# Rotary embedding from cached tables on one core: one of three table copies goes from GpSimd to ScalarE

## The chip, the cores and the metric

One core of a Trainium2 chip. The metric is the device time of one execution in microseconds; the median of several runs is quoted. In the profile, PE is TensorE (PEld its weight loads), DVE is VectorE, ACT is ScalarE, POOL is GpSimd and SP is SyncE. A line number such as L109 is a line of that kernel's source. The change adds one line, so L161 of the kernel before is L162 after it, while L106 to L159 are the same in both.

## The reference

```python
# x: (8, 8, 1024, 64) float32; cos, sin: (1024, 32) float32
half = x.shape[-1] // 2
x_first, x_second = x[..., :half], x[..., half:]
out_first  = x_first * cos - x_second * sin
out_second = x_first * sin + x_second * cos
return concatenate([out_first, out_second], axis=-1)
```

About 17 MB come in and 17 MB go out, with four products and two sums for each pair of elements.

## The kernel before

The input is cut into eight units of 128 partitions x 64 rows x 64 elements (2 MB each). For most units ScalarE stages a piece of x into PSUM, VectorE multiplies it with both tables at once, and GpSimd or TensorE forms the sums; SyncE issues the stores.

The part that matters here is the start. The tables are 1024 rows long. A partition needs 64 of them, an even and an odd block of 32 rows, and the pattern repeats every 16 partitions. In the tile `tb` the odd blocks (rows `H:`) are made for the first 32 partitions by a shuffle, and the same 32 x 2048 numbers are then copied to the other three groups of 32 partitions (the quadrants). The even blocks are spread by TensorE into PSUM (`en` for sin, `ec` for cos), and unit 0's first half is computed straight from there.

```python
for part, r in ((en[:, :BK], rs[:, :BK]), (en[:, BK:], rs[:, BK:]),
                (ec[0], rc[:, :BK]), (ec[1], rc[:, BK:])):
    nc.tensor.matmul(part, sel, r, start=True, stop=True)
odd = [2 * (i % (Q // 2)) + 1 for i in range(Q)]
for t, r in ((sn, rs), (cs, rc)):
    nc.vector.stream_shuffle(t[0:Q, H:], flat(r), odd)
for k in range(1, P // Q):                                   # L160: three copies on GpSimd
    nc.gpsimd.tensor_copy(out=tb4[k * Q:(k + 1) * Q, H:], in_=tb4[0:Q, H:])   # L161
mul(nc.vector, rows(sv[0], 0, H), rows(xt[0], 0, H), tab(flat(en), 0, H))     # x * sin
for i in range(2):                                                            # x * cos
    mul(nc.vector, rows(sv[7], i * G, (i + 1) * G), rows(xt[0], i * G, (i + 1) * G),
        tab(flat(ec[i]), 0, G))
pool_sums(0, 0, H, sv[7])        # GpSimd: reads the sin and the cos products (L109, L110)
stage(pre, 0, H, R)              # ScalarE: second half of unit 0 into PSUM (L113)
nc.scalar.copy(out=sn[:, :H], in_=flat(en))
# ... cos likewise ...
products(pre, 0, H, R)           # VectorE: reads the odd blocks (L106)
pool_sums(0, H, R)               # GpSimd: reads that product
# ... units 1 to 7; in the traces POOL's instructions start in this order ...
```

## Time and profile before

| | before |
|---|---|
| median, lowest to highest of 3 runs | 85.48 us, 85.44 to 85.49 |
| span of the profiled run | 83.3 us |
| busy: DVE, POOL, ACT | 68.5, 69.0, 38.8 us |
| three copies on POOL (L161) | 5.7 us, 1888 ns each |
| POOL's last sum ends | 75.4 us |
| last store lands (issued at 75.88, 6.4 us to landing) | about 82.3 us |

Read it in this order. The busy shares and the 40 slices say which engines are full and when. The chain that ended last says what the profile takes for the path. The order of instructions in a short stretch then shows what really follows on what: the time at which an instruction starts, set against the ends of everything that it reads. The lines themselves are in the prediction below.

### The profile page before, as it was taken

The page shows a single profiled execution, that of the slowest core. Times are in us where ns is not written, and L with a number is a line of the kernel's source. Part 1 is how long each engine was busy: PE and PEld are TensorE (multiplying, and loading weights), DVE is VectorE, ACT ScalarE, POOL GpSimd, SP SyncE. Part 2 cuts the span into 40 slices and gives each one's busy share as a digit, 9 for nine tenths or more (in the row PEclk, how much of TensorE's full clock was granted, in tenths as well). Part 3 has the DMA queues.
Part 4 walks back from the last instruction along what each step waited for, and adds up shares of the span by engine and source line. Part 5 has one row for each costly group of instructions (what it writes and reads, how often), then busy time and mean ns, then how long its engine had stood idle before and what let it go on. Part 6 is the DMA issues. An engine that isn't in the chain of part 4 may idle for free.

```text
span 83.3 us, 386 instructions
## 1 busy us (share of the span) xinstructions
PE 44.0 (53%) x80; PEld 16.9 (20%) x80; DVE 68.5 (82%) x30; ACT 38.8 (47%) x35; POOL 69.0 (83%) x37
## 2 busy tenths in 40 slices
PE   0199930003992694949869494970994970000000
PEld 0143300002440332404233240410430510000000
DVE  0193999999999999999999999999999998950000
ACT  4400795364068548196176856665356627000000
POOL 3009989999999999999999999999999999992000
PEclk9999999999999999999999999999579999755555
DMA  2999999899998999989999999999999999998991
GB/s 35 291 421 456 433 401 480 378 480 401 401 480 378 496 385 409 472 378 496 370 409 472 393 472 409 433 433 401 480 393 464 417 417 448 401 472 373 425 414 71
DMA packets 2832, 33.82 MB, mean 406 GB/s; under 512 B 336, under 2 KB 336, under 8 KB 784
## 3 DMA queue, kind: packets, MB, share of 16 engines
q1 hardware_dynamic: 2784, 33.69, 96.1%
q10 hardware_dynamic: 48, 0.13, 0.4%
HBM read 17.04 MB, written 16.78 MB: 406 GB/s over the span
## 4 chain that ended last, share of the span: by engine, by line
POOL 66%; issue 11%; PE 5%; DMA 4%; DVE 3%; POOLq 2%
POOL w L110 26%; POOL w L109 24%; POOL w L106 14%; PE en L156 5%; DMA w<-in_sin_cached_dram 4%; DVE w L106 3%; POOL tb L161 2%; POOLq L257 2%; POOLq L109 0%; POOLq L106 0%
## 5 line engine op out<-in xcount | busy, mean ns | idle before, releaser
L106 DVE TENSOR_TENSOR w<-st,tb 128x3072 f32<-128x3072 f32 (+2 forms) x19 | 54.7, 2956 | 0.3 <-ACT st L113 0.3
L113 ACT COPY st<-w 128x1536 f32<-128x1536 f32 (+1 forms) x19 | 24.9, 1310 | 15.7 <-DVE w L106 14.8
L183 PE MATMUL acc<-w,plus 128*128 128x512 f32 x36 | 21.3, 677 | 20.4 <-ACT w L189 11.5
L109 POOL TENSOR_TENSOR w<-w 128x1024 f32<-128x1024 f32 (+3 forms) x11 | 23.8, 2165 | 0.2
L110 POOL TENSOR_TENSOR w<-w 128x1024 f32<-128x1024 f32 (+3 forms) x11 | 23.8, 2163 | 0.0
L183 PEld LDWEIGHTS acc<-w,plus 128*128 128x128 f32 x36 | 7.0, 215 | 33.8 <-ACT w L189 18.1
L189 ACT COPY w<-acc 128x1024 f32<-128x1024 f32 x9 | 9.1, 1010 | 8.4 <-PE acc L184 8.4
L106 POOL TENSOR_TENSOR w<-w,tb 128x1280 f32<-128x1280 f32 x4 | 11.6, 2902 | 0.2
L184 PE MATMUL acc<-w,minus 128*128 128x512 f32 x18 | 10.8, 686 | 0.0
L161 POOL COPY tb<-tb 32x2048 f32<-32x2048 f32 x3 | 5.7, 1888 | 5.2 <-DVE tb L159 5.1
L184 PE MATMUL acc<-w,plus 128*128 128x512 f32 x18 | 9.2, 592 | 0.0
L156 PE MATMUL en<-w,sel 32*128 32x512 f32 x4 | 3.7, 1089 | 3.9 <-DMA w<-in_sin_cached_dram 3.9
L184 PEld LDWEIGHTS acc<-w,minus 128*128 128x128 f32 x18 | 4.0, 223 | 5.4 <-issue 5.4
L113 ACT COPY pre<-w 128x2048 f32<-128x2048 f32 x1 | 1.9, 1870 | 5.9 <-DMA w<-in_x_dram 5.9
L106 DVE TENSOR_TENSOR w<-pre,tb 128x4096 f32<-128x4096 f32 x1 | 4.4, 4418 | 0.0
L184 PEld LDWEIGHTS acc<-w,plus 128*128 128x128 f32 x18 | 3.4, 190 | 4.3 <-issue 4.3
L156 PE MATMUL ec<-w,sel 32*128 32x512 f32 x4 | 3.6, 1056 | 0.0
L106 DVE TENSOR_TENSOR w<-w,en 128x2048 f32<-128x2048 f32 x1 | 2.3, 2289 | 1.4 <-PE en L156 1.4
L159 DVE LOAD_MASK_SELECT tb<-w x2 | 0.0, 8 | 3.8 <-DMA w<-in_sin_cached_dram 3.8
L109 POOL TENSOR_TENSOR w<-w,w 128x1024 f32<-128x1024 f32 x1 | 2.3, 2340 | 0.3 <-POOL tb L161 0.3
L159 DVE STREAM_SHUFFLE tb<-w 32x1024 f32<-32x1024 f32 x2 | 2.5, 1278 | 0.0
L106 DVE TENSOR_TENSOR w<-w,ec 128x1024 f32<-128x1024 f32 x2 | 2.4, 1218 | 0.0
(17 smaller groups left out, 12.4 us busy)
## 6 DMA issues: line engine op xcount, KB each, us to landing
w<-in_x_dram SPq DMA_DIRECT2D x7, 2048.0 KB, 24.8
out_dram<-w SPq DMA_DIRECT2D x7, 2048.0 KB, 10.3
w<-in_x_dram SPq DMA_DIRECT2D x2, 1024.0 KB, 6.2
out_dram<-w SPq DMA_DIRECT2D x2, 768.0 KB, 6.4
out_dram<-w SPq DMA_DIRECT2D x1, 512.0 KB, 6.4
w<-in_cos_cached_dram ACTq DMA_DIRECT2D x1, 128.0 KB, 3.4
w<-in_sin_cached_dram SPq DMA_DIRECT2D x1, 128.0 KB, 3.0
```

Source lines behind the costliest of these rows:

```text
L106: eng.tensor_tensor(out=o, in0=a, in1=t, op=TT.mult)
L109: eng.tensor_tensor(out=o[:, :, 0], in0=c[:, :, 0], in1=s[:, :, 1], op=TT.subtract)
L110: eng.tensor_tensor(out=o[:, :, 1], in0=c[:, :, 1], in1=s[:, :, 0], op=TT.add)
L113: nc.scalar.copy(out=pt[:, :(n1 - n0) * hd], in_=xt[u][:, n0 * hd:n1 * hd])
L156: nc.tensor.matmul(part, sel, r, start=True, stop=True)
L159: nc.vector.stream_shuffle(t[0:Q, H:], flat(r), odd)
L161: nc.gpsimd.tensor_copy(out=tb4[k * Q:(k + 1) * Q, H:], in_=tb4[0:Q, H:])
L183: nc.tensor.matmul(a[:, k], plus, xr[:, :, k], start=True, stop=False)
L184: nc.tensor.matmul(a[:, k], plus if k else minus, sr[:, :, 1 - k], start=False, stop=True)
L189: nc.scalar.copy(out=rows(xt[u], n0, n0 + G), in_=a)
L257: with _tile.TileContext(nc) as tc:
```

## The change

Its intent is to take 1.9 us from GpSimd, which is as full as any engine, and give it to ScalarE, which is idle half of the time.

```diff
         for t, r in ((sn, rs), (cs, rc)):
             nc.vector.stream_shuffle(t[0:Q, H:], flat(r), odd)
-        for k in range(1, P // Q):
+        nc.scalar.copy(out=tb4[Q:2 * Q, H:], in_=tb4[0:Q, H:])
+        for k in range(2, P // Q):
             nc.gpsimd.tensor_copy(out=tb4[k * Q:(k + 1) * Q, H:], in_=tb4[0:Q, H:])
```

## The prediction

> **What bounds the kernel now.** I read the page first (engine shares, the 40 slices, the chain), then the busy time by stretch, then the order of the instructions between 3 and 17 us, where the change lies. The page's engine and slice lines:
>
> ```profile
> PE 44.0 (53%) x80; PEld 16.9 (20%) x80; DVE 68.5 (82%) x30; ACT 38.8 (47%) x35; POOL 69.0 (83%) x37
> DVE  0193999999999999999999999999999998950000
> POOL 3009989999999999999999999999999999992000
> DMA  2999999899998999989999999999999999998991
> ```
>
> DVE and POOL are both full from about 8 us to about 75 us, and DMA is full from 2 us to 81 us. Three resources are tied, so 83% on POOL alone doesn't make POOL the bound. The chain that ended last does name POOL (66% of the span), and it holds one piece of the line that changes:
>
> ```profile
> 7.68 2.54 DVE w L106 x2
> 10.23 0.04 issue
> 10.27 1.90 POOL tb L161
> 12.17 0.29 issue
> 12.46 0.03 POOL w L109
> ```
>
> This reads as if the third POOL copy (L161) were on the path. The trap is the 0.29 us of "issue" behind it: the copy has ended at 12.17, and POOL still starts its next work only at 12.46. So something else lets it go. The view of that line (L109) between 5 and 14 us has it:
>
> ```profile
> L109 POOLq EVENT_SEMAPHORE  x2: 17/2940/5863, 6.5 to 12.5; - x2
> its engine sat idle before it (us, times) until:
>   POOL tb L161: 0.3, 1
> ```
>
> POOL's sequencer sits in one semaphore wait for 5.863 us from 6.5 us, that is until about 12.37, and a second one of 17 ns follows. If the copies' end (12.17) were the last thing awaited, the long wait would be over by about 12.2. What does end just before 12.37 is on DVE:
>
> ```profile
> 7.68 2.29 DVE L106 TENSOR_TENSOR w<-w,en 128x2048 f32<-128x2048 f32 x1 [1.42 <-PE en L156]
> 9.88 2.43 DVE L106 TENSOR_TENSOR w<-w,ec 128x1024 f32<-128x1024 f32 x2
> 12.23 4.42 DVE L106 TENSOR_TENSOR w<-pre,tb 128x4096 f32<-128x4096 f32 x1
> ```
>
> 9.88 + 2.43 = 12.31 us is the end of the two products by cos, and L109 is the sum that reads exactly these (the compiled order shows L109 waiting on a DVE semaphore as well as on POOL's own). 12.31 plus about 0.06 is 12.37. The view's "POOL tb L161" is an inferred releaser; the times speak for DVE.
>
> The end of the run has a second lock. Busy POOL time, DMA share and rate by stretch, from 44 us on:
>
> ```profile
> 44.00:48.00 4.00, 4.00 (x4) 1.00 0.96 410
> 52.00:56.00 4.00, 4.00 (x3) 1.00 1.01 430
> 64.00:68.00 4.00, 4.00 (x2) 1.00 0.97 414
> 72.00:75.40 3.40, 3.40 (x2) 0.50 0.97 414
> 75.40:81.40 6.00, 0.03 (x1) 0.50 0.99 413
> ```
>
> Columns: the stretch, its length, POOL's busy time, the granted clock, DMA share, GB/s. DMA never falls below 0.96 although stores come only as the sums finish. After POOL has ended (75.4), DMA works 6 us more at its full rate. It moves 413 GB/s x 6.0 us = 2.48 MB there (and about 0.08 MB in the tail), while the two stores not yet issued at 75.4 are 768 KB and 512 KB, 1.31 MB. So some 1.25 MB, about 3 us, of older stores are still queued when POOL delivers its last sum.
>
> **What the Trainium skill says.** "ScalarE: Activation LUTs", section "What ACT_TABLE_LOAD costs": an instruction with immediate scale and bias takes 186 ns + 0.833 ns per element of the row, 1892 ns at 2048. The trace agrees: ACT's 128x2048 copy takes 1870 ns. "GPSIMD Engine Reference", section "Engine selection": one-input work on POOL is roughly line-rate, so ACT should not be a faster copier. It agrees: L161 takes 1888 ns for 32x2048. "SBUF — State Buffer", section "SBUF: two separate sides": DVE and GpSimd share one port pair, ACT has its own; a DVE operation with two SBUF inputs can be blocked by POOL. No such block shows here: DVE's products have one input in PSUM, and the 1024-wide product takes 1218 ns beside POOL's copy and 1222 to 1224 ns beside POOL's sums. "DMA: Bandwidth & Descriptors", section "Where 436 GB/s comes from": a ceiling of 435 GB/s for the 16 engines. The trace holds 410 to 446 GB/s in every stretch that I read between 6.4 and 75 us, at about that ceiling; the page's lower HBM limit, about 358, doesn't show.
>
> **The change part by part.** Removed from POOL: one of three copies of 32x2048, 1.89 us. The order stays otherwise the same: on POOL two copies and then the same 28 sums and products. POOL's copies would run from 6.41 to 6.41 + 2 x 1.89 = 10.2 instead of 12.17. Then L109 still waits for DVE's second cos product (12.31) and starts at 12.46 as before. So 1.89 us of busy time becomes 1.9 us more of idle time (0.3 to about 2.2 us), and the path gains nothing.
>
> Added on ACT: one copy of the same size, about 1.87 us, ahead of the staging of the first unit's second half. It waits for the second shuffle (4.99 + 1.28 = 6.27 us), so it runs from about 6.4 to 8.3. ACT is idle there: the staging starts only at 8.91, because its data comes with a DMA (5.9 us of idle time "<-DMA w<-in_x_dram"). It fits with about 0.6 us to spare. Were it late, the staging (8.91 + 1.87 = 10.78) still has 1.45 us until DVE takes it up at 12.23.
>
> Moved on DVE: nothing. Its big product at 12.23 reads the table that these copies write, but it starts 0.08 us before the recorded end of the product ahead of it, just as the next one does (16.57 against 12.23 + 4.42 = 16.65). That is the back-to-back cadence, not a wait. Earlier copies release nothing there.
>
> Sum on the path: POOL 0, DVE 0, ACT 0, DMA 0. The median stays at 85.48; I say 85.45.
>
> **The rivals.** (1) POOL's whole chain moves up by 1.89 us and the time follows, to about 83.6. For it: the chain view and POOL's 83%. Against it: the DVE product at 12.31. Even if it held, the last sums read DVE's product that ends at 58.00 + 12.07 = 70.07, so POOL could finish no earlier than about 70.1 + 1.8 + 1.8 = 73.7 (now 75.4): 1.7 us at most, before the DMA. (2) POOL moves up and the stores hide it: the 3 us queued at the end swallow the 1.7 us, and the time is the same. I hold the first lock to act already, with this one behind it. (3) ACT becomes late and holds DVE back. That needs the staging to slip by 1.45 us; a copy about twice as long, 4 us, would do it, and then the time would rise by a few tenths at most before DMA's queue hides it too. Nothing in the rows of ACT's copies (1.0 us for 1024, 1.87 for 2048) points to that. (4) DVE runs faster with POOL silent between 10.2 and 12.3. If the second cos product became shorter, L109 would start earlier by as much; but its 1218 ns equals the width-1024 product elsewhere, so at most 0.05 us.
>
> **Range and chances.** All paths lead to the same time; what remains is the scatter between chips and calls. The three runs lie within 0.05 us, and I allow some 0.3% (0.25 us) each way for another chip: 85.2 to 85.7. Faster by 2% would need 83.8 us, which the DMA queue and the DVE gate both exclude: 2%. Slower by 2% would need 1.7 us of new delay, against slacks of 0.6 and 1.45 us: 2%.
>
> **What would show it.** Right: in the changed kernel two POOL copies end near 10.2, L109 still starts within 0.1 us of 12.46 with about 2.2 us of idle time in front of it, its releaser now a DVE product; ACT's new copy lies between 6.3 and 8.4, and its staging starts again near 8.9; POOL still ends near 75.4, with busy time 1.9 us lower; DMA share stays near 1 up to 81.4. Wrong: L109 starting near 10.4 (the sum does not wait for DVE), the ACT copy taking over 3 us, or its staging starting later than 9. The prediction as a whole fails if the DMA rate moves, since 1% of it is 0.8 us.

## The result, and the profile after

The median is 85.30 us (85.14 to 85.43, 6 runs) beside 85.49 us for the kernel before (85.44 to 85.70, 6 runs). The ratio is 0.9973, with a 95% interval of 0.9959 to 0.9987. A ratio here is the mean time of one kernel's fast runs over that of the other's fast runs of the same rounds, so it is not quite the ratio of the medians.

The engine line and three slice lines of the page after, to set against those of before:

```profile
PE 44.1 (53%) x80; PEld 16.9 (20%) x80; DVE 68.5 (82%) x30; ACT 40.7 (49%) x36; POOL 67.2 (80%) x36
...
DVE  0193999999999999999999999999999998940000
POOL 3009909999999999999999999999999999991000
...
DMA  1999999999999999999999898999999999999990
```

POOL has lost 1.8 us of busy time and ACT has gained 1.9. The DVE line is as before but for one digit near the end (5, now 4). In POOL's line a hole has opened in the sixth slice (10.4 to 12.5 us) where an 8 stood, and its last busy slice is the same one (2, now 1; the last sum ends at 75.50 instead of 75.43): the work taken away has left a gap.

The order of instructions of the kernel after, between 6 and 13 us, some of it (start, duration, engine, line; in brackets the idle time ahead and what ended it):

```profile
6.34 1.90 ACT L160 COPY tb<-tb 32x2048 f32<-32x2048 f32 x1 [3.36 <-DVE tb L159]
6.46 3.82 POOL L162 COPY tb<-tb 32x2048 f32<-32x2048 f32 x2 [5.15 <-DVE tb L159]
...
9.12 1.87 ACT L113 COPY pre<-w 128x2048 f32<-128x2048 f32 x1 [0.88 <-DMA w<-in_x_dram]
...
9.92 2.43 DVE L106 TENSOR_TENSOR w<-w,ec 128x1024 f32<-128x1024 f32 x2
...
12.27 4.42 DVE L106 TENSOR_TENSOR w<-pre,tb 128x4096 f32<-128x4096 f32 x1
12.49 2.36 POOL L109 TENSOR_TENSOR w<-w,w 128x1024 f32<-128x1024 f32 x1 [2.22 <-issue]
```

POOL's copies end at 10.28, and the next sum still starts at 12.49 (12.46 before). The idle time ahead of it is 2.22 us instead of 0.29. The profile can't name its releaser any more and says "issue". The view of L109 between 5 and 16 us has the wait itself (shortest/median/longest in ns, then the first and the last start in us):

```profile
L109 POOLq EVENT_SEMAPHORE  x2: 17/2884/5750, 6.6 to 12.5; - x2
```

It ends at the same place as before, although the copies ended 1.9 us earlier. The end of the run is unchanged too. Stretch, length, POOL's busy time, granted clock, DMA share and GB/s, after:

```profile
75.40:81.40 6.00, 0.11 (x1) 0.50 1.00 419
```

### The profile page after: what moved, and what is told of

Same layout as the page of the kernel before. It is cut to its first block, busy times and chain, and to the rows that moved or that the text cites. A ratio compares the mean times of both kernels' runs of the same rounds, so it can differ in the third digit from the quotient of the medians.

```text
span 83.6 us, 386 instructions
## 1 busy us (share of the span) xinstructions
PE 44.1 (53%) x80; PEld 16.9 (20%) x80; DVE 68.5 (82%) x30; ACT 40.7 (49%) x36; POOL 67.2 (80%) x36
## 3 DMA queue, kind: packets, MB, share of 16 engines
HBM read 17.04 MB, written 16.78 MB: 404 GB/s over the span
## 4 chain that ended last, share of the span: by engine, by line
POOL 63%; issue 13%; PE 4%; DMA 4%; DVE 3%; POOLq 2%
POOL w L109 26%; POOL w L110 24%; POOL w L106 14%; PE en L156 4%; DMA w<-in_sin_cached_dram 4%; DVE w L106 3%; POOLq L258 2%; POOLq L109 0%; POOLq L106 0%
## 5 line engine op out<-in xcount | busy, mean ns | idle before, releaser
L109 POOL TENSOR_TENSOR w<-w 128x1024 f32<-128x1024 f32 (+3 forms) x11 | 23.9, 2169 | 0.2
L162 POOL COPY tb<-tb 32x2048 f32<-32x2048 f32 x2 | 3.8, 1888 | 5.2 <-DVE tb L159 5.2
L109 POOL TENSOR_TENSOR w<-w,w 128x1024 f32<-128x1024 f32 x1 | 2.4, 2361 | 2.2 <-issue 2.2
L160 ACT COPY tb<-tb 32x2048 f32<-32x2048 f32 x1 | 1.9, 1897 | 3.4 <-DVE tb L159 3.4
```

The source lines that it names most:

```text
L109: eng.tensor_tensor(out=o[:, :, 0], in0=c[:, :, 0], in1=s[:, :, 1], op=TT.subtract)
L160: nc.scalar.copy(out=tb4[Q:2 * Q, H:], in_=tb4[0:Q, H:])
```

## The experiments

Twelve kernels were run, each beside the kernel before on the same chip. Four calls of the kernel before have medians of 85.31 to 85.49 us, so each ratio below is taken within its own rounds. A run more than 1.5% above the fastest of its kernel counts as slow and is left out of the ratios.

**Is there a small gain? null and again.** `null` is the kernel before with one comment line added; `again` is the changed kernel once more, with no edit.

```diff
+        # nothing changed
         odd = [2 * (i % (Q // 2)) + 1 for i in range(Q)]
```

> The kernel before with one comment line added: no instruction differs. It measures what two identical kernels differ by in the same rounds. If the 0.27% by which the changed kernel was faster (ratio 0.9973, interval 0.9959 to 0.9987) is scatter of placement and rounds, this null ratio lies up to 0.3% from 1 too. If the 0.27% is a real gain, the null is within 0.1% of 1.0000 and the repeat of the changed kernel is again near 0.997.

> The changed kernel once more, 5 rounds. Theory (POOL waits for DVE's cos product at 12.3 us, the copy saved turns into idle time, nothing on the path moves): ratio 0.998 to 1.002, POOL's first sum at 12.4 to 12.6 us with 2.2 us of idle time ahead of it. Rival (a small real gain of 0.2 us from POOL being quiet between 10.2 and 12.3 us): ratio near 0.9973 again, below the null by 0.2% or more.

`null`: 85.48 us, ratio 1.0002 (0.9977 to 1.0027). `again`: 85.28 us, ratio 0.9981 (0.9955 to 1.0007), POOL's first sum at 12.47 us after 2.22 us idle. The expectations don't settle the last 0.2%: two identical kernels can differ by a quarter of a per cent by the width of the null's interval, and the repeat's interval holds 1, but both sets of runs of the changed kernel came out 0.2 us lower. Within the same rounds the mean of `again` is 0.19 us below that of `null`. So is that of `nogate` below (0.20 us), where POOL isn't quiet between 10.3 and 12.3 us; so that quiet isn't needed for it.

**Is it the POOL copy? dummy1.** The changed kernel gets one useless copy on POOL, into part of a buffer that nobody reads before it is overwritten.

```diff
             nc.gpsimd.tensor_copy(out=tb4[k * Q:(k + 1) * Q, H:], in_=tb4[0:Q, H:])
+        for k in range(1, 2):
+            nc.gpsimd.tensor_copy(
+                out=sv[3][k * Q:(k + 1) * Q, :2 * C].rearrange(
+                    "p (n t j) -> p n t j", t=2, j=half), in_=tb4[0:Q, H:])
```

> The changed kernel with one useless POOL copy of 32x2048 put after its two real ones (into a quarter of a buffer that nobody reads), so that POOL is as busy as before while ACT still does its copy. Theory: it fills the idle 2.2 us (1.89 us of it), POOL's first sum still starts at 12.4 to 12.6 us, and the time is that of the changed kernel within 0.2%. Rival (saving the POOL copy was worth something of its own): slower than the changed kernel by what was gained, 0.2 us, or by up to 1.7 us if POOL's copies were on the path.

It took 85.43 us, ratio 0.9995 (0.9970 to 1.0019). POOL's first sum started at 12.46 with 0.28 us of idle time ahead, so the extra copy went into the gap:

```profile
12.46 2.35 POOL L109 TENSOR_TENSOR w<-w,w 128x1024 f32<-128x1024 f32 x1 [0.28 <-POOL w L164]
```

The view names the useless copy (L164) as the releaser, though the sum reads nothing that it writes. A whole 1.89 us of POOL work at this place is worth nothing that could be told from zero: 1.7 us is excluded. The median is 0.15 us above that of `again`, which fits both what was expected (within 0.2%) and the rival's 0.2 us.

**What does POOL wait for? nogate.** POOL's first sum reads the unit's input instead of DVE's products, and writes to a buffer that is overwritten later. Its output is wrong, which doesn't matter for the time.

```diff
-        pool_sums(0, 0, H, sv[7])
+        sums(nc.gpsimd, rows(sv[5], 0, H), rows(xt[0], 0, H), rows(xt[0], 0, H))
```

> The changed kernel, but POOL's first sum reads the unit's input instead of DVE's two cos products and writes into a buffer that is overwritten later (so half of the first unit is wrong on purpose); same size, same place in POOL's order. Theory: the DVE product is what POOL waits for, so the first sum now starts near 10.3 to 10.5 us instead of 12.49. Then a second gate holds POOL: the next sum reads DVE's big product, which ends at 16.7, so POOL starts it near 16.8 instead of 17.09, and its chain ends only some 0.25 us earlier (75.2 instead of 75.5); time unchanged within 0.3%. Rival (POOL waits for its own copies or for a load): the first sum starts at 12.4 as before. Rival (POOL's chain is free to move once the first gate is open): POOL ends 2 us earlier and the time falls by up to 1.7 us.

85.32 us, ratio 0.9978 (0.9955 to 1.0002). The view of L109 between 5 and 16 us in this run:

```profile
L109 POOLq EVENT_SEMAPHORE  x2: 17/17/17, 6.4 to 10.2; - x2
```

POOL's order of instructions from 10 to 19 us:

```profile
10.27 2.34 POOL L109 TENSOR_TENSOR w<-w 128x1024 f32<-128x1024 f32 x1
12.57 2.33 POOL L110 TENSOR_TENSOR w<-w 128x1024 f32<-128x1024 f32 x1
16.68 2.35 POOL L109 TENSOR_TENSOR w<-w 128x1024 f32<-128x1024 f32 x1 [1.78 <-DVE w L106]
```

The long wait is gone (17 ns is the longest left), and the sum starts at 10.27, right after the copies. So DVE's products were what POOL waited for: removing the dependence on them (the reads, and the overwriting of the input that they read) opens the gate. Then the second gate shows as forecast. POOL idles 1.78 us until DVE's big product is over, and starts the second sum at 16.68 instead of 17.09. POOL's last sum ends at 75.27 (75.50 after the change). The 2 us have shrunk to 0.2.

**How much delay of POOL does the end hide? dummy2 and dummy3.** As `dummy1`, with two and three useless copies.

```diff
-        for k in range(1, 2):
+        for k in range(1, 3):      # dummy2;  range(1, 4) in dummy3
```

> The changed kernel with two useless POOL copies after its two real ones. Now POOL's copies should end at 6.4 + 4 x 1.9 = 14.1, past the DVE product at 12.3, so POOL's own work gates the first sum: it starts near 14.2, and all of POOL's chain lies 1.7 us later (last sum ends near 77.1). DMA theory: the last 768 KB store took 6.4 us from issue to landing; a 128 KB load on an empty queue took 3.0, so 768 KB alone would take about 3.0 + 640 KB / 425 GB/s = 4.6 us (estimate from these rows); the queue at the end thus hides some 1.8 us, and 1.7 us more on POOL costs 0 to 0.4 us. Rival (POOL's chain sets the end): 1.7 us slower (2.0%).

> Three useless POOL copies: POOL's chain 3.6 us later (first sum near 16.1, last sum ends near 79.0). DMA theory: the 1.8 us that the queue hides are used up, so the time rises by 3.6 - 1.8 = 1.8 us, to about 87.1 (1.4 to 2.3 us). Rival (POOL's chain sets the end): 3.6 us slower, 88.9. Rival (DMA total alone sets it, whatever POOL does): unchanged.

| | POOL's first sum | POOL's last sum ends | time, ratio to before (95%) |
|---|---|---|---|
| again (no useless copy) | 12.47 us | 75.40 us | 85.28, 0.9981 (0.9955 to 1.0007) |
| dummy1 | 12.46 | 75.44 | 85.43, 0.9995 (0.9970 to 1.0019) |
| dummy2 | 14.18 | 77.08 | 85.43, 1.0016 (0.9978 to 1.0054) |
| dummy3 | 16.07 | 79.00 | 86.62, 1.0153 (1.0111 to 1.0195) |

POOL's chain moves as a whole by 1.7 and 3.6 us, so the shift is carried to its end. (The profile of `dummy2` is of its slowest run, 85.87 us.) The time moves by 0.14 us (within noise) and 1.3 us. This is the reverse of the change and tells more: POOL can be 1.7 us late without a cost that could be told from zero, and at 3.6 us late some 2.3 us are still hidden (1.9 to 2.7 by the ratio's interval). I had expected 1.8 us to be hidden and the time to rise by 1.4 to 2.3 us, so 1.3 us is just outside; the size was off by 0.5 us, the mechanism held. The second half of the mechanism is in the DMA columns of `dummy3` (stretch, length, busy PE, PEld, DVE, ACT and POOL, clock, DMA share, GB/s):

```profile
66.00:76.00 10.00, 2.32 (x6) 0.76 (x4) 7.69 (x6) 1.93 (x2) 10.00 (x6) 0.86 0.91 387
76.00:78.00 2.00, 0.00 (x0) 0.00 (x0) 0.00 (x0) 0.00 (x0) 2.00 (x2) 0.50 0.93 393
```

The share falls to 0.91 over 10 us, where the kernel before holds 1.01 from 66 to 74 us and 0.99 from 74 to 76. The queue does run dry once POOL is 3.6 us late: from 67.35 to 68.25 us the windows view of `dummy3` has a DMA share of 0.00, that of `dummy2` 0.98 and that of the kernel before 1.15. The other sign of used-up slack is the time from the end of POOL's last sum to the end of the span: 7.9 us before, 8.1 after the change, 6.7 in `dummy2`, 5.7 in `dummy3`. It is 5.7 in `lessdma` below too, where less is stored instead, so about 8.1 - 5.7 = 2.4 us can be hidden. From issue to landing the 768 KB stores took 4.2 us (median) in both of these runs, 6.4 before.

**How much can ScalarE take? act2 and act3.** ScalarE makes two, or all three, of the copies.

```diff
-        nc.scalar.copy(out=tb4[Q:2 * Q, H:], in_=tb4[0:Q, H:])
-        for k in range(2, P // Q):
+        for k in range(1, 3):      # act2;  range(1, 4) in act3
+            nc.scalar.copy(out=tb4[k * Q:(k + 1) * Q, H:], in_=tb4[0:Q, H:])
+        for k in range(3, P // Q): # act2;  no copy left for GpSimd in act3
             nc.gpsimd.tensor_copy(out=tb4[k * Q:(k + 1) * Q, H:], in_=tb4[0:Q, H:])
```

> ScalarE makes two of the three copies, POOL one. Theory: ACT's copies run 6.3 to 10.1, so they are over 1 us past the arrival of the load that ACT's staging waited for; the staging runs 10.1 to 12.0 and is just ready for DVE's product at 12.25. Nothing on the path moves: 85.2 to 85.6. Rival (ACT is already at its limit, any more delays DVE): DVE's product starts 0.5 us later or more.

> ScalarE makes all three copies, POOL none. Theory: ACT's copies run 6.3 to 12.0, staging ends near 13.9, DVE's product starts near 13.9 instead of 12.25, so DVE's and POOL's later work lies 1.5 to 1.7 us later; POOL's first sum still at 12.45, since that waits for the cos product only. The DMA queue at the end hides about 1.8 us, so the time rises by 0 to 0.5 us. Rival (DVE and POOL set the end): 1.6 us slower.

`act2`: 85.63 us, ratio 1.0032 (1.0001 to 1.0064). `act3`: 85.51 us, ratio 1.0031 (0.9982 to 1.0079). `act2` came out just above the expected 85.2 to 85.6. In it the staging ran 10.06 to 11.91 and DVE's product started at 12.28 without idling, as forecast. In `act3` ACT, POOL and DVE, each from its own order of instructions, read:

```profile
6.21 5.71 ACT L161 COPY tb<-tb 32x2048 f32<-32x2048 f32 x3 [3.25 <-DVE tb L159]
11.84 1.85 ACT L113 COPY pre<-w 128x2048 f32<-128x2048 f32 x1
...
12.31 2.32 POOL L109 TENSOR_TENSOR w<-w,w 128x1024 f32<-128x1024 f32 x1 [11.02 <-DVE w L106]
...
13.72 4.42 DVE L106 TENSOR_TENSOR w<-pre,tb 128x4096 f32<-128x4096 f32 x1 [1.50 <-ACT pre L113]
```

Two things are to be seen. POOL has no copy at all, idles for 11.02 us, and its first sum starts at 12.31, as ever, now with DVE named as the releaser. And DVE really waits for ScalarE, by 1.50 us, yet the time rises by 0.3% only, which its interval can't tell from zero. POOL's last sum ended at 76.80 there instead of 75.50, so a late DVE is hidden at the end as a late POOL is. In `act2` POOL works 1.9 us less than in the changed kernel and the time is not lower but slightly higher, which also speaks against quiet on POOL as the source of the 0.2 us of the first section.

**Does an earlier POOL ever pay? lightpool, lessdma and both.** Their outputs are wrong, which doesn't matter for the times. `lightpool` leaves out one sum of unit 1 (two operations, 4.7 us). `lessdma` stores 8 of unit 0's 64 rows only. `both` does both.

```diff
-        2: [(pool_sums, 1, 32, 64), (on_pool, 2, K // 2, K)],     # lightpool, both
+        2: [(on_pool, 2, K // 2, K)],
-    store(0)                                                      # lessdma, both
+    store(0, 0, 8)
```

> The changed kernel with one POOL sum of the second unit left out (two operations of 128x1024, 4.7 us; half of that unit is wrong on purpose). POOL's chain is now free to move by 4.7 us after the first gates, until its last pair meets DVE's product that ends at 70.1: POOL ends near 73.7 instead of 75.5. DMA theory: the queue never ran dry, so the time is unchanged, 85.2 to 85.6. Rival (POOL's chain sets the end): 1.7 us faster, 83.6 to 83.8.

> The changed kernel, but the first unit's store writes only 8 of its 64 rows (1.84 MB less, worth 4.3 us at 425 GB/s; most of that unit is missing on purpose). All engines do the same work. DMA theory: the time falls until the queue has no slack left, by about 2.2 us (what the third useless copy showed to be hidden: 3.5 - 1.3), to about 83.1 (82.8 to 83.6); then POOL's last sum sets the end. Rival (POOL's chain sets the end): unchanged.

> Both at once: less to store and one POOL sum left out. DMA theory: now POOL's chain is what sets the end, so its 1.7 us count in full: about 81.4 (81.1 to 82.0), 1.5 to 1.8 us below the run with less to store alone, although the same omission was worth nothing with the full stores. Rival: if the POOL omission is worth the same in both cases, the two differ by what it was worth alone.

`lightpool`: 85.69 us, ratio 1.0025 (1.0005 to 1.0046): nothing gained, as forecast, though 0.09 us above the expected range. But POOL's last sum ended at 76.51 in the profiled run, not at 73.7. That run had a lower granted TensorE clock (0.891 of full speed, the others 0.914 to 0.918), its DVE was over 1 us late when it came to unit 6, and POOL idled 1.86 us for it. `lessdma`: 82.90 us, ratio 0.9698 (0.9682 to 0.9714), 2.6 us faster with the engines' work unchanged; one run of 84.59 was slow. `both`: a miss. I expected 81.4; the two fast runs were 82.97 and 84.09, two more were slow (84.83 and 85.97), and why this kernel scatters so was not found. Its time proves nothing. Its trace does tell why the omission bought nothing. Two lines of POOL's order in `both` and the matching one in `lessdma`:

```profile
54.81 3.41 POOL L109 TENSOR_TENSOR w<-w 128x1536 f32<-128x1536 f32 x1 [2.41 <-DVE w L106]
...
63.54 2.36 POOL L109 TENSOR_TENSOR w<-w 128x1024 f32<-128x1024 f32 x1 [1.91 <-DVE w L106]
```

```profile
63.63 2.45 POOL L109 TENSOR_TENSOR w<-w 128x1024 f32<-128x1024 f32 x1
```

The first of these sums adds the products of unit 5, the second those of unit 6, both made by DVE. With 4.7 us less to do, POOL idles for 2.41 and 1.91 us in front of them and starts the second at 63.54, against 63.63 in `lessdma` without the omission. So of the 4.7 us only 0.09 are left at 63.5 us. Even with fewer stores, POOL's 4.7 us turn into waiting for DVE, and what the kernel then runs into is DVE's pace.

**A version that is faster? tables.** The changed kernel, with the sin load issued by ScalarE ahead of the cos load, so that SyncE can start on x at once.

```diff
-    nc.sync.dma_start(out=rs, in_=sin_cached.rearrange("(q n) j -> q (n j)", q=Q))
+    nc.scalar.dma_start(out=rs, in_=sin_cached.rearrange("(q n) j -> q (n j)", q=Q))
     nc.scalar.dma_start(out=rc, in_=cos_cached.rearrange("(q n) j -> q (n j)", q=Q))
```

> Tried for a faster version: the changed kernel with the sin table's load issued by ScalarE ahead of the cos table's, so that SyncE issues the first load of x at about 0.74 instead of 1.18 us. If DMA is the bound from the first load to the last store, starting its stream 0.4 us sooner is worth up to 0.4 us (85.0). Against it: the tables may now land later behind x's packets, which delays DVE and POOL, and the last sums with them; 2.2 us of that is hidden. I expect 84.9 to 85.5.

86.51 us, ratio 1.0130 (1.0108 to 1.0153): slower, outside my range. The DMA issues of this run (KB each, microseconds from issue to landing):

```profile
w<-in_sin_cached_dram ACTq DMA_DIRECT2D x1, 128.0 KB, 4.5
w<-in_cos_cached_dram ACTq DMA_DIRECT2D x1, 128.0 KB, 7.7
```

Before, these took 3.0 and 3.4 us. SyncE did issue x at 0.74, but the cos table now landed at 8.85 us behind x's packets, and DVE's big product started at 14.48 instead of 12.27. The first 30 us also moved fewer bytes (416 GB/s from 6 to 30 us, 433 in the changed kernel); why was not tried. No version that computes the right result beats both kernels.

## Why the prediction was right or wrong

The measured 85.30 us lies in the range of 85.2 to 85.7, 0.1 us from its lower edge, and the time stayed within 2%, as forecast with 96%. The 0.2 us that brought it near the edge was not foreseen and is not explained.

- **The gate at 12.3 us.** Right, and shown: the first sum started at 12.49 with two copies, at 12.31 with none, at 12.46 with a useless third, and at 10.27 as soon as it no longer read DVE's products. The reading that carried it was that the end of the long wait (12.37) fitted DVE's end (12.31) plus 0.06 us and not the copy's end (12.17). One sign failed: the view was to name a DVE product as the releaser, and it says "issue"; it names DVE only in `act2` and `act3`.
- **ScalarE's copy fits.** Right. It took 1.90 us (1.87 forecast), from 6.34 to 8.24. The criterion "staging later than 9" was set too sharply: it started at 9.12. ACT idled 0.88 us in front of it for the load, so the load was late and not the copy; in `null`, without any such copy, it started at 9.04. The 1.45 us of slack behind the staging was right too: with two copies on ScalarE DVE didn't wait, with three it waited 1.50 us.
- **Nothing moves on DVE.** Right: same busy time and nearly the same gaps; its big product started at 12.27 (12.23).
- **The second lock, DMA.** Right in kind. The 3 us of queued stores are not all usable. At 3.6 us of delay 2.3 us were hidden (`dummy3`), and `lessdma` gained 2.6 us of the 4.3 us that the bytes were worth; both end 5.7 us after POOL's last sum, and that part can't be hidden. I take what is missing from the 3 us to be the fixed time of a new store (a 128 KB load took 3.0 us to land, though its bytes are worth only 0.3 us at 425 GB/s); that is argued, not tried.
- **The floor in the first rival was wrong.** I put POOL's earliest end at 73.7 us, from DVE's product that ends at 70.07. The step missed the sum of unit 6 ahead of it, which reads DVE products that end near 63.5 us, when POOL comes to it at 63.7 anyway. POOL's earliest end is about 75.2, as `both` showed with 75.18. The first rival would thus have given 0.2 us and not 1.7. It also missed a nearer gate: POOL's second sum reads the product that ended at 16.65 and started at 17.04, so no more than 0.4 us could be won there, and `nogate` won 0.2. The miss came back in what I expected of `lightpool` and `both`.
- **The DMA rate was misread.** "410 to 446 GB/s in every stretch" doesn't hold for the stretches that were read: 68 to 72 us had 451, and short ones of 0.3 to 2 us had 164 to 504. Over 6 to 75.4 us the rate was 430. Nothing in the forecast hung on it.
- **The 0.2 us.** The forecast of 85.45 was 0.15 us above the median. Two sets of runs put the changed kernel 0.2% to 0.3% lower; no start or end in the traces moves that way, and the null can't exclude scatter. It stays open.

## What to carry to other kernels

When an instruction starts later than the end of its named releaser, look for another input that ends just before the start: here 0.29 us of unexplained idle time was the first sign that told a useful saving from a useless one, and the end of one semaphore wait the second. An engine that is 83% busy and on the chain may still only follow another engine; ask of every later gate too, since work taken off POOL came back as waiting at 12.3, 16.7, 54.8 and 63.5 us. Where the DMA queue is full to the end, first measure how much delay it hides by adding useless work; here that gave the slack (2.3 us) that no single trace line showed.

## What the Trainium skill lacked or had wrong

- "DMA: Bandwidth & Descriptors", section "Where 436 GB/s comes from", says that for transfers between HBM and SBUF the HBM side (~358 GB/s) binds. That can't be taken for a core that works alone: the changed kernel, on one core, moved 429 GB/s of loads and stores from 6 to 75.4 us. The page's own measured table, which is for a single core, has 425 GB/s at 16 MB; the sentence doesn't say which case it is for.
- The same page, section "Issuing engines are not separate DMA queues", says that issuing from several engines only saves sequencer time. It has no figure for what a small load pays beside large ones: the same 128 KB load landed in 3.4 us issued from ScalarE first, and in 7.7 us issued second with x already on SyncE's queue, and the kernel was 1.3% slower.
- "GPSIMD Engine Reference", section "Engine selection", calls one-input work roughly line-rate, and the page has no measured time of a copy: a 32x2048 float32 copy took 1888 ns on GpSimd and 1897 ns on ScalarE, so moving it there gains nothing in itself.
- "Perfetto Trace Analysis", section "Identifying Dependency Chains", says to read which semaphores an instruction waits for, but not how to test which of several came last when a profile infers a releaser. The wait of 5.86 us in GpSimd's sequencer, ending at 12.37 us where the copies had ended at 12.17, was what told it.
